# Two of four chunk pairs of each FFN's first product as seven block products instead of eight

## The chip, the cores and the metric

The kernel runs on one core of a Trainium2 chip. The metric is the device time of one execution in microseconds (us). Before the change it was 1284.43 us, the median of three runs (1284.11 to 1285.47).

## The reference

A decoder trunk of two layers on 256 tokens of width 1024, all in float32. Each layer is an FFN, a mixer of three branches, and a second FFN, each between two RMS norms:

```
def swiglu(h, wi, wo):
    gate, up = jnp.split(h @ wi, 2, axis=-1)
    return (jax.nn.silu(gate) * up) @ wo

for l in range(DEPTH):          # DEPTH = 2
    h = rms_norm(x, ffn1_pre_g[l])
    x = x + 0.5 * rms_norm(swiglu(h, ffn1_wi[l], ffn1_wo[l]), ffn1_post_g[l])
    h = rms_norm(x, mix_pre_g[l])
    y = hybrid_mixer(h, w_in[l], ...)
    x = x + rms_norm(y, mix_post_g[l])
    h = rms_norm(x, ffn2_pre_g[l])
    x = x + 0.5 * rms_norm(swiglu(h, ffn2_wi[l], ffn2_wo[l]), ffn2_post_g[l])
```

The change is in the product `h @ wi`, which stands in four FFN stages: (256 x 1024) by (1024 x 5632).

## The kernel before, in words

**Precision.** Every float32 operand of a large product is split into a high part (a cast to fp32r) and a low part (the operand minus the high part). A product is then three matmuls: high by high, low by high, high by low (`mm3`, L289 to L293). The activations' parts are `hh` and `hl`, made once a stage. The weights' parts are `hi` and `lo`, made as the weights come in: ScalarE casts (L146), VectorE subtracts (L147).

**Units.** The weights lie packed in 212 units of 128 x 2048 floats (1 MB) in the order of their use. A unit has two halves of 128 x 1024. `dma_to` loads a unit into one of two `raw` tiles, on the SyncE queue in order. `splitter` splits a half when one of eight ring places for hi and lo is free (`RING = 8`, `st_["free"]`), and `release` frees a place once PE's matmuls on that half have been issued. Two units at a stage boundary have tiles of their own (`place`, tag `q4`).

**An FFN stage.** The 5632 columns of wi are eleven chunks of 256 gate and 256 up columns. `wi(us, j, tt, rel)` makes chunk j for one half of the tokens (tt = 0 or 1, 128 tokens): `chunk512` multiplies the eight blocks of 128 rows, 24 matmuls of 128x512, into one PSUM bank of the pool `pmm`, which has two banks in turn. A coroutine then does silu on ScalarE (L349), the product with the up half on VectorE (L350), two transposes on PE (L237), and the split of the transposed result (L230 on ScalarE, L231 on VectorE) into `gT`. `wo(unit, j, tt, rel)` multiplies gT of chunk j with the rows of wo into two accumulators `acc`, 12 matmuls. In the middle of the stage the order is: wo of chunk j-2 for both token halves (one unit, freed in its second half), then wi of chunk j for both (two units, freed in the second). So a chunk is 72 matmuls of 128x512 and four transposes.

**Order.** The program is written by coroutines that run on a virtual clock (`Clock`): PE's instructions advance it, and the splitter and the gates yield a number of virtual microseconds. A scheduler then fixes each engine's order at build time from the program order, priorities (`tc.high_priority`) and its own estimates. On the chip each engine works through its list in order, and waits at an instruction whose inputs or whose tile are not there yet.

Of the kernel before, what the change touches and what calls it, by code (L numbers as in the profile page):

```python
# [15 lines left out]
P = 128  # L16
# [18 lines left out]
def f32(ap):  # L35
    return ap.bitcast(F32)
# [40 lines left out]
def trunk(ctx, tc, x, wpk, gains, lnp, wst, bst, consts, out, depth=DEPTH):  # L77
# [38 lines left out]
            tc.add_manual_dep(i.ins, lastdma[0].ins.name, NOSYNC, reason="load order")  # L116
        lastdma[0] = i

    def dma_to(n):
        while st_["dma"] < min(n, NU):  # L120
            u = st_["dma"]
            t = rp.tile([P, 2048], F32, tag="raw", name=f"raw{u}", bufs=2)
            for q in range(2 if u == 0 else 1):
                c = slice(1024 * q, 1024 * q + 1024) if u == 0 else slice(0, 2048)
                load(t[:, c], wpk[u][:, c])
            raws[u] = t
            st_["dma"] += 1

    def splitter():
        for u in range(NU):  # L130
            dma_to(u + 2)
            halves[u] = []
            for q in range(2):
                gate = place.get(u)
                while st_["free"] <= 0 if gate is None else not gate.on:
                    yield 0.2
                    gate = place.get(u)
                if gate is not None:
                    h = sp.tile([P, 1024], F32R, tag="q4", name=f"hi{u}_{q}", bufs=9)
                    lo = sp.tile([P, 1024], F32R, tag="q4", name=f"lo{u}_{q}", bufs=9)  # L140
                else:
                    st_["free"] -= 1
                    h = rp.tile([P, 1024], F32R, tag="hi", name=f"hi{u}_{q}", bufs=RING)
                    lo = rp.tile([P, 1024], F32R, tag="lo", name=f"lo{u}_{q}", bufs=RING)
                r = raws[u][:, 1024 * q:1024 * q + 1024]
                S.copy(h, r)  # L146
                V.tensor_sub(lo, r, f32(h))  # L147
                halves[u].append((h, lo))
                yield 1.2

    def wcols(u, c, n):
        h, lo = halves[u][c // 1024]
# [3 lines left out]
    def take(n):  # L156
        u0 = st_["pos"]
        st_["pos"] += n
        return list(range(u0, u0 + n))
# [23 lines left out]

    load(xs[0], x[0:P, :])
    gain(0)
    dma_to(1)
    load(xs[1], x[P:SEQ, :])
    dma_to(2)

    mB_ = cp.tile([P, 1152], BF16, tag="mB", name="mB")  # L190
    mB = [mB_[:, 768:1152], mB_[:, 0:768]]
# [94 lines left out]
            hready[tt] = f  # L286
            yield from prenorm(tt, nxt, f)

    def mm3(o, ah, al, bh, bl, first, stop, n=512):  # L289
        T.matmul(o, ah, bh, start=first, stop=False)  # L290
        T.matmul(o, ah, bl, start=False, stop=False)  # L291
        T.matmul(o, al, bh, start=False, stop=stop)  # L292
        ck.pe(3 * (n / 2400 + 0.003))  # L293

    def chunk512(us, tt, rel):
# [36 lines left out]
    def ffn(gi, nxt, first):  # L332
        acc = [None, None]
        gT, gf = {}, {}
        always = Flag()
        always.on = True
        for i in (32, 33):
            place[st_["pos"] + i] = always

        def wi(us, j, tt, rel):  # L340
            ps = chunk512(us, tt, rel)
            if tt == 0:
                t = sp.tile([P, 2, NT, 2, P], F32R, tag="t4", name=nm("gT"), bufs=5)
                gT[j] = (t[:, 0], t[:, 1])
            f = gf[j, tt] = Flag()

            def co():
                sg = w3_tile("sg")
                S.activation(sg[:, 0:256], ps[:, 0:256], AF.Silu)  # L349
                V.tensor_mul(sg[:, 0:256], ps[:, 256:512], sg[:, 0:256])  # L350
                yield 4.5 if (j, tt) == (0, 0) else 2.0
                to_T(sg, tt, 0, 2, *gT[j])
                yield 1.0
                f.on = True

            c = co()
            ck.start(c, 0.2)

        def wo(unit, j, tt, rel):
            ck.until(lambda: gf[j, tt].on)  # L360
            if acc[tt] is None:
                acc[tt] = [sc_tile("acc"), sc_tile("acc")]
            if j == NCH - 1:
                finish(tt, gi + 1, acc[tt], unit, *gT[j], 0, 2 * j, 2 * NCH, rel, 0.5, nxt)
            else:
                kunit(acc[tt], unit, *gT[j], tt, 0, 2 * j, 2 * NCH, rel)

        ua, ub = take(2), take(2)
        order = ((ua, 0, 0), (ua, 0, 1), (ub, 1, 0), (ub, 1, 1)) if first else \
                ((ua, 0, 0), (ub, 1, 0), (ua, 0, 1), (ub, 1, 1))  # L370
        for w, j, tt in order:
            wi(w, j, tt, tt == 1)
        for j in range(2, NCH - 1):
            if j == 3:
                if first:
                    load_consts()
                gain(gi + 1)
                gain(gi + 2)
            uo = take(1)[0]
# [444 lines left out]
```

## Time and profile before

| what | value |
|---|---|
| median of three runs | 1284.43 us |
| the profiled execution | 1285.66 us, its span 1284.0 us |
| PE busy | 1270.5 us (99%), 6428 matmuls |
| VectorE (DVE) busy | 763.0 us (59%) |
| ScalarE (ACT) busy | 645.5 us (50%) |
| DMA | 234.21 MB, mean 182 GB/s |
| mean granted TensorE clock | 0.999 |

The span is the time from the first to the last instruction of the profiled execution; the execution itself is 1.7 us longer. PE's matmuls overlap, so the busy time of one (about 0.39 us for 128x512) is not its cost: the distance of two start times is. The four FFN stages lie at about 12 to 190, 468 to 635, 635 to 823 and 1112 to 1278 us of the span, the mixers between them.

### The profile page before, as it was taken

How to read it: one execution, taken by the hardware profiler on the slowest of the kernel's cores; microseconds unless marked ns; L12 is line 12 of the kernel's file. 1: busy time of each engine (PE TensorE's matmuls, PEld its weight loads, DVE VectorE, ACT ScalarE, POOL GpSimd, SP SyncE). 2: the span in 40 equal slices, each digit the busy share in tenths (PEclk: the TensorE clock that was granted, in tenths of full speed). 3: DMA queues.
4: the chain of work that ended last, by engine and by line, in shares of the span. 5: the costliest groups of instructions: out<-in, count | busy, mean ns of one | idle time of the engine just before them, and what ended most of it. 6: DMA issues, size and time to landing. Idle time of an engine off the chain costs nothing.

```text
span 1284.0 us, 16016 instructions
## 1 busy us (share of the span) xinstructions
PE 1270.5 (99%) x6428; PEld 1059.2 (82%) x6428; DVE 763.0 (59%) x957; ACT 645.5 (50%) x896; POOL 34.5 (3%) x81
## 2 busy tenths in 40 slices
PE   8999999999999999999999999999999999999998
PEld 6888887998778888888888888789977788888886
DVE  5655557546765965555665555775466568655553
ACT  5544455445666454444554444654366655544442
POOL 0000001000000010000000000010000000000000
PEclk9999999999999999999999999999999999999999
DMA  7765554555335546555545555544543355455551
GB/s 246 262 225 192 176 189 163 197 190 190 116 125 193 200 161 230 197 182 182 179 177 212 185 194 197 197 170 166 213 167 131 131 197 201 160 212 178 185 179 50
DMA packets 34922, 234.21 MB, mean 182 GB/s; under 512 B 4128, under 2 KB 4256, under 8 KB 7840
## 3 DMA queue, kind: packets, MB, share of 16 engines
q1 hardware_dynamic: 34848, 233.20, 51.5%
q8 instruction: 50, 0.82, 0.3%
q14 instruction: 24, 0.20, 0.0%
HBM read 232.13 MB, written 1.05 MB: 182 GB/s over the span
## 4 chain that ended last, share of the span: by engine, by line
PE 95%; DVE 2%; ACT 2%; DMA 1%; issue 0%; SPq 0%; POOL 0%; DVEq 0%; POOLq 0%; ACTq 0%
PE mm L290 18%; PE mm L292 18%; PE mm L291 18%; PE acc L292 6%; PE acc L291 6%; PE acc L290 6%; PE qk L292 3%; PE qk L291 3%; PE qk L290 3%; PE tr L237 3%; PE pj L292 1%; PE pj L290 1%; PE pj L291 1%; PE wo L292 1%; PE wo L290 1%; PE wo L291 1%
## 5 line engine op out<-in xcount | busy, mean ns | idle before, releaser
L147 DVE TENSOR_TENSOR lo<-raw,hi 128x1024 fp32r<-128x1024 f32 x424 | 512.2, 1223 | 210.9 <-ACT hi L146 197.2
L146 ACT CAST hi<-raw 128x1024 fp32r<-128x1024 f32 x424 | 439.5, 1050 | 240.3 <-PE mm L292 86.2
L290 PE MATMUL mm<-hi,hh 128*128 128x512 f32 x1024 | 408.6, 399 | 1.4 <-ACT hh L230 1.4
L292 PE MATMUL mm<-hi,hl 128*128 128x512 f32 x1024 | 400.9, 391 | 0.2 <-DVE hl L231 0.2
L291 PE MATMUL mm<-lo,hh 128*128 128x512 f32 x1024 | 400.4, 391 | 0.0
L290 PEld LDWEIGHTS mm<-hi,hh 128*128 128x128 f32 x1024 | 193.1, 189 | 42.2 <-issue 2.7
L292 PEld LDWEIGHTS mm<-hi,hl 128*128 128x128 f32 x1024 | 192.8, 188 | 41.8 <-DVE hl L231 0.9
L291 PEld LDWEIGHTS mm<-lo,hh 128*128 128x128 f32 x1024 | 193.2, 189 | 36.7
L290 PE MATMUL acc<-hi,gT 128*128 128x512 f32 x352 | 140.9, 400 | 0.0
L292 PE MATMUL acc<-hi,gT 128*128 128x512 f32 x352 | 137.7, 391 | 0.0
L291 PE MATMUL acc<-lo,gT 128*128 128x512 f32 x352 | 137.3, 390 | 0.0
L349 ACT ACTIVATE sg<-mm 128x256 f32<-128x256 f32 x88 | 33.7, 383 | 160.8 <-PE mm L292 160.4
L350 DVE TENSOR_TENSOR sg<-mm,sg 128x256 f32<-128x256 f32 x88 | 37.0, 420 | 117.8 <-ACT sg L349 117.8
L290 PE MATMUL qk<-hh,hi 128*128 128x256 f32 x320 | 91.2, 285 | 0.0
L292 PE MATMUL qk<-hh,lo 128*128 128x256 f32 x320 | 90.6, 283 | 0.0
L291 PE MATMUL qk<-hl,hi 128*128 128x256 f32 x320 | 90.6, 283 | 0.0
L230 ACT CAST gT<-tr 128x256 fp32r<-128x256 f32 x88 | 32.4, 368 | 98.0 <-PE tr L237 98.0
L292 PEld LDWEIGHTS acc<-hi,gT 128*128 128x128 f32 x352 | 66.1, 188 | 14.1 <-DVE gT L231 0.2
L291 PEld LDWEIGHTS acc<-lo,gT 128*128 128x128 f32 x352 | 66.3, 188 | 12.5
L290 PEld LDWEIGHTS acc<-hi,gT 128*128 128x128 f32 x352 | 66.2, 188 | 12.3
L231 DVE TENSOR_TENSOR gT<-tr,gT 128x256 fp32r<-128x256 f32 x88 | 37.0, 421 | 63.1 <-ACT gT L230 63.0
L291 PEld LDWEIGHTS qk<-hl,hi 128*128 128x128 f32 x320 | 61.4, 192 | 0.1
(138 smaller groups left out, 1051.2 us busy)
## 6 DMA issues: line engine op xcount, KB each, us to landing
raw<-wpk SPq DMA_DIRECT2D x211, 1024.0 KB, 4.9
gain<-gains SPq DMA_DIRECT2D x12, 512.0 KB, 6.8
x<-x SPq DMA_DIRECT2D x2, 512.0 KB, 5.9
raw<-wpk SPq DMA_DIRECT2D x2, 512.0 KB, 6.9
ln<-lnp SPq DMA_DIRECT2D x4, 256.0 KB, 5.6
out<-x SPq DMA_DIRECT2D x4, 256.0 KB, 2.0
ws<-wst SPq DMA_DIRECT2D x2, 256.0 KB, 5.9
cst<-consts SPq DMA_DIRECT2D x1, 384.0 KB, 5.4
```

The costliest lines, as they stand in the source:

```text
L146: S.copy(h, r)
L147: V.tensor_sub(lo, r, f32(h))
L230: lasthi[0] = S.copy(h_out, src)
L231: V.tensor_sub(l_out, src, f32(h_out))
L237: T.transpose(tr[:, k * P:(k + 1) * P], src[:, k * P:(k + 1) * P], ident)
L290: T.matmul(o, ah, bh, start=first, stop=False)
L291: T.matmul(o, ah, bl, start=False, stop=False)
L292: T.matmul(o, al, bh, start=False, stop=stop)
L349: S.activation(sg[:, 0:256], ps[:, 0:256], AF.Silu)
L350: V.tensor_mul(sg[:, 0:256], ps[:, 256:512], sg[:, 0:256])
```

## The change

For the chunk pairs (4, 5) and (8, 9) of each stage the activations A (two token halves by two halves of the 1024 rows) and the weights B (two halves of the rows by two chunks) are taken as 2 x 2 blocks. The block product is made with Winograd's form of Strassen's scheme: seven products of 12 matmuls (`prod`) instead of eight. It needs four sums of activation blocks (`sums`, once a stage, on VectorE, then split), four sums of weight blocks a pair (made by the splitter on VectorE, eight sums of 128x1024, then split like weights), and five combinations of PSUM results (`post`, VectorE, 128x512). Product 1 is copied from PSUM by ScalarE, and the results of the bank of products 2 and 4 are added to that copy.

The loader follows a list `plan`. In a pair it has nine units to split where there were six: B11, T2, wo, B21, T3, T1, wo, T4, B22. B11 and B12 are loaded into four `q4` tiles, where T1 and T3 are made in place. T2 and T4 are made in two tiles of the tag `xn`. Block B22 is loaded twice. The activation sums have four `q4` tiles for the stage. In `pair7` two PSUM banks of `pmm` are used as b0 and b1; products 1 and 3, 2 and 4, 5 and 7 share a bank, product 6 has one.

```diff
+QUADS = (4, 8)
...
+            plan += [("w", c(j, q)) for j in range(2) for q in range(2)]
+            for j in range(2, NCH - 1, 2):
+                if j in qj:
+                    k = Quad({}, c(j, 0), c(j, 1), c(j + 1, 0), c(j + 1, 1))
...
+                    plan += [("B11", k), ("T2", k), ("w", w(j - 2)), ("B21", k), ("T3", k), ("T1", k),
+                             ("w", w(j - 1)), ("T4", k), ("B22", k)]
...
+        def stream(key, u, first=False):
+            while len(ring) >= 2 and ring[-2] not in done:
+                yield
+            ring.append(key)
             t = rp.tile([P, 2048], F32, tag="raw", name=f"raw{u}", bufs=2)
...
+            if kind == "B11":
+                f = k.ffn
+                if "f" not in f:
+                    f["f"] = [sp.tile([P, 1024], F32, tag="xn", name=nm("wf"), bufs=2) for _ in WQ]
+                for q in range(2):
+                    V.tensor_add(f["a"][q], f["a"][q], f["b"][q])
+                    V.tensor_add(f["f"][q], f["a"][q], raw[k][q])
+                    yield 1.2
+            elif kind == "T2":
+                for q in range(2):
+                    V.tensor_add(k.ffn["b"][q], k.ffn["b"][q], raw[k][q])
+                    yield 0.6
+                done.add(k)
+            elif kind == "B21":
+                for q in range(2):
+                    V.tensor_add(k.ffn["f"][q], k.ffn["f"][q], raw[n][q])
+                    yield 0.6
...
+        def sums(ss):
+
+            def full(tt, k):
+                t = w3_tile("sA")[:, 0:512].rearrange("p (k t) -> p k t", t=P)
+                V.tensor_add(t, f32(hh[:, tt, k:k + 4, :]), f32(hl[:, tt, k:k + 4, :]))
+                return t
+
+            def split(a):
+                o = sp.tile([P, 2, 4, P], F32R, tag="q4", name=nm("sA"), bufs=9)
+                S.copy(o[:, 0], a)
+                V.tensor_sub(o[:, 1], a, f32(o[:, 0]))
+                ss.append(o)
...
+        def prod(ps, ah, al, it, first):
+
+            for k in range(4):
+                have(it, k // 2)
+                h, l = wcols(it, k * 512, 512)
+                mm3(ps, ah[:, k, :], al[:, k, :], h, l, first and k == 0, k == 3, go_on=not first)
+                if k % 2:
+                    release(it)
...
+            def post(o, a, b, op):
+                with tc.high_priority(offset=HOT):
+                    V.tensor_tensor(o, a, b, op=op)
...
+            def chunk(jj, tt, a, b, op):
+                c = w3_tile("cc")
+                post(c[:, 0:512], a, b, op)
+                out(c[:, 0:256], c[:, 256:512], jj, tt, c[:, 0:256])
+
+            b0, b1 = mm(), mm()
+            prod(b0, *A(0, 0), take(1)[0], True)
+            S.copy(p1, b0)
+            prod(b1, *s2, take(1)[0], True)
+            post(u2, b1, p1, ALU.add)
+            wo2(j - 2)
+            prod(b0, *A(0, 4), take(1)[0], False)
+            out(b0[:, 0:256], b0[:, 256:512], j, 0, w3_tile("sg")[:, 0:256])
+            prod(b1, *s3, take(1)[0], False)
+            post(u3, b1, p1, ALU.add)
+            b0 = mm()
+            prod(b0, *s1, take(1)[0], True)
+            chunk(j + 1, 1, b0, u3, ALU.subtract)
+            wo2(j - 1)
+            b1 = mm()
+            prod(b1, *A(1, 4), take(1)[0], True)
+            chunk(j, 1, b1, u3, ALU.add)
+            prod(b0, *s4, take(1)[0], False)
+            chunk(j + 1, 0, b0, u2, ALU.subtract)
```

`out` is the gate of `wi` (silu, product, transposes, split) as a function of its own. The consts and two gains are loaded at chunk 4 instead of 3.

How the order moves, first on PE at the end of the last pair before chunk 10 in the second FFN. `mm` are banks of `pmm` (every second number is the same bank), `sA` the sums of activations, `tr` a transposed tile, `cc` a combined chunk. Before:

```order
L290 MATMUL mm_373_4952<-hi100_1_4859,hh_94 128x512
L291 MATMUL mm_373_4952<-lo100_1_4860,hh_94 128x512
L292 MATMUL mm_373_4952<-hi100_1_4859,hl_95 128x512
L290 MATMUL mm_376_4999<-hi101_0_4871,hh_94 128x512
L291 MATMUL mm_376_4999<-lo101_0_4872,hh_94 128x512
L292 MATMUL mm_376_4999<-hi101_0_4871,hl_95 128x512
```

and now:

```order
L383 MATMUL mm_400_5048<-hi112_1_5057,sA_350_4217 128x512
L384 MATMUL mm_400_5048<-lo112_1_5058,sA_350_4217 128x512
L385 MATMUL mm_400_5048<-hi112_1_5057,sA_350_4217 128x512
L383 MATMUL mm_408_5171<-hi113_0_5069,hh_94 128x512
L384 MATMUL mm_408_5171<-lo113_0_5070,hh_94 128x512
L385 MATMUL mm_408_5171<-hi113_0_5069,hl_95 128x512
L330 MATMUL tr_409_5175<-ident_73,cc_406_5143 128x128 x2
```

Before, chunk 10 took the bank of mm_371, which was filled one whole product before mm_373. Now mm_408 takes the bank of mm_400 (mm_405, product 6, has the other), which is filled by the three rows just above it.

Second, VectorE at the same place, before (chunk 9 and the splits of chunk 10; `sg` is a gate):

```order
L231 TENSOR_TENSOR gT_365_4830<-tr_368_4854,gT_365_4830 128x256
L147 TENSOR_TENSOR lo101_0_4872<-raw101_4813,hi101_0_4871 128x1024
L350 TENSOR_TENSOR sg_369_4881<-mm_366_4831,sg_369_4881 128x256
L147 TENSOR_TENSOR lo101_1_4885<-raw101_4813,hi101_1_4884 128x1024
L231 TENSOR_TENSOR gT_365_4830<-tr_370_4902,gT_365_4830 128x256
```

and now, from the combination of product 6 on:

```order
L536 TENSOR_TENSOR cc_406_5143<-mm_405_5120,u_393_4912 128x512
L218 TENSOR_TENSOR lo115_0_5137<-raw103_5094,hi115_0_5136 128x1024
L470 TENSOR_TENSOR cc_406_5143<-cc_406_5143 128x256
L218 TENSOR_TENSOR lo115_1_5151<-raw103_5094,hi115_1_5150 128x1024
L536 TENSOR_TENSOR cc_407_5169<-mm_400_5048,u_393_4912 128x512
L324 TENSOR_TENSOR gT_399_5024<-tr_409_5175,gT_399_5024 128x256
L470 TENSOR_TENSOR cc_407_5169<-cc_407_5169 128x256
```

Two combinations (L536) stand among the splits (L218); the second, cc_407, is what reads product 7 out of its bank.

Third, VectorE in the first FFN, at chunk 2 (unit 9 is the last of chunk 3, `wa` holds B11 of the first pair). Before:

```order
L147 TENSOR_TENSOR lo8_1_404<-raw8_344,hi8_1_403 128x1024
L350 TENSOR_TENSOR sg_33_435<-mm_30_399,sg_33_435 128x256
L147 TENSOR_TENSOR lo9_0_445<-raw9_371,hi9_0_444 128x1024
L147 TENSOR_TENSOR lo9_1_460<-raw9_371,hi9_1_459 128x1024
L231 TENSOR_TENSOR gT_31_430<-tr_34_454,gT_31_430 128x256
```

and now:

```order
L218 TENSOR_TENSOR lo8_1_427<-raw8_344,hi8_1_426 128x1024
L504 TENSOR_TENSOR sA_41_444<-sA_41_444,sA_34_392 128x512
L218 TENSOR_TENSOR lo9_0_477<-raw9_375,hi9_0_476 128x1024
L218 TENSOR_TENSOR lo9_1_492<-raw9_375,hi9_1_491 128x1024
L218 TENSOR_TENSOR lo10_0_504<-wa_29_377,hi10_0_503 128x1024
L488 TENSOR_TENSOR sA_33_389<-sA_28_363,sA_33_389 128x512
L488 TENSOR_TENSOR sA_38_419<-sA_34_392,sA_38_419 128x512
L488 TENSOR_TENSOR sA_40_441<-sA_27_361,sA_40_441 128x512
L488 TENSOR_TENSOR sA_42_459<-sA_41_444,sA_42_459 128x512
L443 TENSOR_TENSOR sg_45_467<-mm_39_422,sg_45_467 128x256
L443 TENSOR_TENSOR sg_47_513<-mm_44_463,sg_47_513 128x256
```

The gate of chunk 2's first token half stood ahead of the splits of unit 9; now it stands behind them, behind a half of B11 and behind the four splits of activation sums.

## Rows read from the trace of the kernel before

**Rows 1.** Page, part 1: busy us of each engine, share of the span, instructions.
```profile
PE 1270.5 (99%) x6428; PEld 1059.2 (82%) x6428; DVE 763.0 (59%) x957; ACT 645.5 (50%) x896; POOL 34.5 (3%) x81
```

**Rows 2.** Page, part 4: chain that ended last, share of the span by engine.
```profile
PE 95%; DVE 2%; ACT 2%; DMA 1%; issue 0%; SPq 0%; POOL 0%; DVEq 0%; POOLq 0%; ACTq 0%
```

**Rows 3.** Waits of PE: us in total, times, longest.
```profile
PE tr L237 <- DVE sg L350: 2.0, 3, 0.7
PE tr L237 <- DVE xn L258: 1.6, 1, 1.6
PE mm L290 <- ACT hh L230: 1.4, 1, 1.4
```

**Rows 4.** Timeline of PE in an output product: start, us, engine, line, operation.
```profile
516.14 0.39 PE L290 MATMUL acc<-hi,gT 128*128 128x512 f32 x1
...
518.86 0.39 PE L290 MATMUL acc<-hi,gT 128*128 128x512 f32 x1
```

**Rows 5.** Stretches: length, busy us of PE, PEld, DVE, ACT, POOL; PEclk, DMA, GB/s.
```profile
60.00:70.00 10.00, 10.00 (x47) 8.24 (x46) 5.09 (x8) 3.99 (x7) 0.00 (x0) 1.00 0.90 342
...
468.00:635.00 167.00, 167.00 (x759) 137.73 (x758) 89.75 (x106) 76.71 (x107) 0.86 (x2) 1.00 0.54 190
...
510.66:527.48 16.82, 16.82 (x77) 13.87 (x76) 8.87 (x10) 7.62 (x11) 0.00 (x0) 1.00 0.55 189
```

**Rows 6.** Timeline of ACT in the second FFN; in brackets idle time, and its end.
```profile
528.84 1.05 ACT L146 CAST hi<-raw 128x1024 fp32r<-128x1024 f32 x1 [0.98 <-PE mm L292]
530.20 1.05 ACT L146 CAST hi<-raw 128x1024 fp32r<-128x1024 f32 x1 [0.30 <-PE mm L292]
```

**Rows 7.** Groups by line and shape: busy us, mean ns | idle before, releaser.
```profile
L147 DVE TENSOR_TENSOR lo<-raw,hi 128x1024 fp32r<-128x1024 f32 x424 | 512.2, 1223 | 210.9 <-ACT hi L146 197.2
L146 ACT CAST hi<-raw 128x1024 fp32r<-128x1024 f32 x424 | 439.5, 1050 | 240.3 <-PE mm L292 86.2 <-PE qk L291 61.7 <-DMA raw<-wpk 41.2
...
L231 DVE TENSOR_TENSOR gT<-tr,gT 128x256 fp32r<-128x256 f32 x88 | 37.0, 421 | 63.1 <-ACT gT L230 63.0
L350 DVE TENSOR_TENSOR sg<-mm,sg 128x256 f32<-128x256 f32 x88 | 37.0, 420 | 117.8 <-ACT sg L349 117.8
L349 ACT ACTIVATE sg<-mm 128x256 f32<-128x256 f32 x88 | 33.7, 383 | 160.8 <-PE mm L292 160.4 <-DVE gT L231 0.3
...
L230 ACT CAST gT<-tr 128x256 fp32r<-128x256 f32 x88 | 32.4, 368 | 98.0 <-PE tr L237 98.0
...
L230 ACT CAST hh<-tr 128x512 fp32r<-128x512 f32 x32 | 18.5, 586 | 30.3 <-PE tr L237 30.3
...
L271 DVE TENSOR_TENSOR yn<-acc,gain 128x512 f32<-128x512 f32 x16 | 11.0, 689 | 16.4 <-ACT sq L270 16.4
...
L690 DVE TENSOR_TENSOR mg<-mg,gate 128x512 f32<-128x512 f32 x16 | 10.6, 682 | 0.0
...
L655 ACT COPY gate<-mm 128x512 f32<-128x512 f32 x12 | 7.0, 583 | 6.9 <-PE mm L292 6.9
```

**Rows 8.** Page, part 6: DMA issues, KB each, median us from issue to landing.
```profile
raw<-wpk SPq DMA_DIRECT2D x211, 1024.0 KB, 4.9
```

**Rows 9.** Timeline of DVE in the first FFN: two splits back to back.
```profile
45.91 2.36 DVE L147 TENSOR_TENSOR lo<-raw,hi 128x1024 fp32r<-128x1024 f32 x2 [0.58 <-ACT hi L146]
```

**Rows 10.** Timeline of ACT in the first FFN.
```profile
41.56 1.05 ACT L146 CAST hi<-raw 128x1024 fp32r<-128x1024 f32 x1 [3.04 <-DMA raw<-wpk]
...
49.16 0.38 ACT L349 ACTIVATE sg<-mm 128x256 f32<-128x256 f32 x1 [2.33 <-PE mm L292]
50.52 1.05 ACT L146 CAST hi<-raw 128x1024 fp32r<-128x1024 f32 x1 [0.98 <-PE mm L292]
```

**Rows 11.** Stretches at a norm boundary and at the end, columns as in rows 5.
```profile
190.00:198.00 8.00, 7.33 (x38) 5.72 (x37) 7.01 (x9) 4.62 (x8) 1.01 (x2) 1.00 0.33 109
...
1276.00:1284.00 8.00, 1.60 (x8) 0.98 (x6) 2.79 (x4) 1.38 (x4) 0.86 (x2) 0.77 0.18 66
```

More of the change, by code (lines that the diff above doesn't have):

```diff
@@ L122, in dma_to, with loader @@
+    NI = len(plan)
+    WQ = (slice(0, 1024), slice(1024, 2048))
+    done, raw = set(), {}
+    def loader():
+        ring = []
+        def stream(key, u, first=False):
+            while len(ring) >= 2 and ring[-2] not in done:
+                yield
+            ring.append(key)
             t = rp.tile([P, 2048], F32, tag="raw", name=f"raw{u}", bufs=2)
-            for q in range(2 if u == 0 else 1):
-                c = slice(1024 * q, 1024 * q + 1024) if u == 0 else slice(0, 2048)
+            raw[key] = [t[:, c] for c in WQ]
+            for c in WQ if first else (slice(0, 2048),):
@@ L125, in dma_to @@
                 load(t[:, c], wpk[u][:, c])
-            raws[u] = t
-            st_["dma"] += 1
+        for n, (kind, k) in enumerate(plan):
+            if kind == "w":
+                yield from stream(n, k, n == 0)
+            elif kind == "B11":
+                while k.prev and not k.prev.t1:
+                    yield
+                f = k.ffn
+                if not f:
+                    for t in "ab":
+                        f[t] = [sp.tile([P, 1024], F32, tag="q4", name=nm("w" + t), bufs=9) for _ in WQ]
+                raw[n] = f["a"]
+                for t, u in ((f["a"], k.u11), (f["b"], k.u12)):
+                    for q, c in enumerate(WQ):
+                        load(t[q], wpk[u][:, c])
+                yield from stream(k, k.u22)
+            elif kind in ("B21", "B22"):
+                yield from stream(n, k.u21 if kind == "B21" else k.u22)
+            yield
@@ L129, in splitter, with ready @@
+    ld = loader()
+    def ready(n, kind, k):
+        if kind[0] == "T":
+            raw[n] = k.ffn[{"T1": "a", "T2": "f", "T3": "b", "T4": "f"}[kind]]
+        return n in raw and (kind != "B11" or k in raw)
     def splitter():
-        for u in range(NU):
-            dma_to(u + 2)
-            halves[u] = []
+        for n, (kind, k) in enumerate(plan):
+            while not ready(n, kind, k):
+                next(ld)
+            halves[n] = []
             for q in range(2):
-                gate = place.get(u)
+                gate = place.get(n)
@@ L151, in wcols @@
+            done.add(n)
+            for _ in range(3):
+                next(ld, None)
     def wcols(u, c, n):
@@ L366, in wo, with out, co @@
                 kunit(acc[tt], unit, *gT[j], tt, 0, 2 * j, 2 * NCH, rel)
+        def out(ps_a, ps_b, j, tt, sg):
+            if j not in gT:
+                t = sp.tile([P, 2, NT, 2, P], F32R, tag="t4", name=nm("gT"), bufs=5)
+                gT[j] = (t[:, 0], t[:, 1])
+            f = gf[j, tt] = Flag()
+            def co():
+                S.activation(sg, ps_a, AF.Silu)
+                V.tensor_mul(sg, ps_b, sg)
+                yield 2.0
+                to_T(sg, tt, 0, 2, *gT[j])
+                yield 1.0
+                f.on = True
+            ck.start(co(), 0.2)
@@ new lines, in sums @@
+        def sums(ss):
[8 more added lines that the diff above has]
+                ss.append(o)
+            t, s1 = full(1, 0), full(1, 4)
+            yield 1.5
+            V.tensor_sub(s1, t, s1)
+            split(s1)
+            s2 = full(0, 0)
+            yield 2.2
+            V.tensor_sub(t, s2, t)
+            V.tensor_sub(s2, s1, s2)
+            split(s2)
+            yield 2.2
+            split(t)
+            s4 = full(0, 4)
+            yield 2.2
+            V.tensor_add(s4, s4, s2)
+            split(s4)
@@ L368, in ffn @@
+        ss = []
         ua, ub = take(2), take(2)
@@ L372, in ffn @@
             wi(w, j, tt, tt == 1)
+        ck.start(sums(ss), 0.2)
         for j in range(2, NCH - 1):
-            if j == 3:
+            if j == 4:
                 if first:
```

75 lines of the change are left out of this document (58 added, 17 removed).

## The prediction

> **What bounds the kernel now.** First the page's table of engines [rows 1]: PE is busy 99% of the span, VectorE 59%, ScalarE 50%. Then the chain that ended last [rows 2]: 95% of it is PE. Then the waits of PE [rows 3]: the three largest entries are 2.0, 1.6 and 1.4 us. So the time is the number of matmuls times their spacing, plus a short start and tail. The spacing is read from the start times in the PE timeline [rows 4]: twelve 128x512 matmuls from 516.14 to 518.86, so 2.72 us for twelve, 0.2267 each (the 0.39 us of one matmul overlaps the next).
>
> Next the room on the other engines in an FFN, from the table by stretches [rows 5]: one output chunk takes 16.82 us, in which PE is always busy, VectorE works 8.87 us and ScalarE 7.62. Last, who holds whom: the casts that start a weight split wait for PE [rows 6], because all eight ring places are full and PE has to free one. So weights are ready four units before their use. That lead is what the change spends.
>
> **What it removes.** A pair of chunks has eight block products of 12 matmuls; the new pair has seven. Two pairs in each of four FFN stages: 8 x 12 = 96 matmuls, 96 x 0.2267 = 21.8 us (2.72 a pair). Transposes and output products stay. A pair goes from 33.6 us (two chunks of rows 5) to 30.9.
>
> The Trainium skill has smaller spacings: "TensorE: Matmul & The Clock Gate", section "Back-to-back issue gap", gives about 131 ns sustained for 512 columns, by which the gain would be 12.6 us. The trace disagrees, with 0.2267 us where PE never waits [rows 4], and the row decides.
>
> **What it adds, per pair.** Seven weight blocks are split where four were: six more casts (1.05 us) and six more subtractions (1.22) [rows 7]. Eight sums of 128x1024 fp32 weights on VectorE are not in the trace. Bounds: 0.68 (the 128x512 sum L690, as if size cost nothing) and 1.36 (that row twice); the subtraction L147 has the same shape and number of operands, so 1.22. Five combinations of a 128x512 PSUM result: 0.69 (L271). One copy of the first product on ScalarE: 0.58 (L655). VectorE in a pair: 9 units x 2 x 1.22 + 8 x 1.22 + 5 x 0.69 + 4 x (0.42 + 0.42) = 22.0 + 9.8 + 3.4 + 3.4 = 38.6 us against 30.9 of PE; before it was 17.7 against 33.6. ScalarE: 18 x 1.05 + 0.58 + 4 x (0.38 + 0.37) = 22.5, which fits. Once a stage the token sums cost VectorE 12 x 0.68 = 8.2 us and ScalarE 4 x 0.59. A whole stage gives VectorE 12 x 1.22 + 16 x 1.22 + 10 x 0.69 + 8.2 = 49 us more; in the stretch 468 to 635 of rows 5 it has 89.8 of 167, so 139 of about 162: 86%.
>
> **Does PE wait for weights?** I keep a ledger from the start of the chunk before a pair to the pair's last product: PE 16.8 + 30.9 = 47.7 us. PE frees 3 + 9 units in it, so VectorE makes 24 splits (29.3), 8 sums (9.8), 5 combinations (3.4) and about six gates with their transposed halves (5.0): 47.5. It breaks even over the stretch. Inside, it falls behind where the four sums after the first block meet the two splits beside them: six operations, 7.3 us, in a 5.4 us output product. Going through the new order by hand with these durations I find it at most about 5 us late. The lead is four units, 10.9 us where all four are product blocks (2.72 each) and more with an output unit. So weights don't stall PE, and the following chunks (8.87 of 16.8) refill the ring. The second block's weights must also follow the sums through a load: block 21 takes the place of block 22 once VectorE has used that, and needs 4.9 us to land [rows 8]; by the ledger VectorE waits 1 to 2 us for it, inside the lead. Block 22 is loaded twice, 1 MB a pair; the queue has brought 342 GB/s where 189 is usual here [rows 5, 8].
>
> **Where PE does wait.** VectorE works in the order it was given, so a combination that PE needs stands behind the splits placed ahead of it. Three places:
> 1. After the second pair's product 7, PE goes straight on with the last chunk's first product, which takes the PSUM bank that product 7 just filled; before, that bank had been read out one 5.4 us product earlier. From the end of product 6 VectorE has a combination, a split, a gate, a split and the last combination: 0.69 + 1.18 + 0.42 + 1.18 + 0.69 = 4.2 us (1.18 is half of two splits back to back, 2.36 us [rows 9]). PE arrives after 2.72: it waits 1.5 us in three stages. In the first stage the order has one split less and no gate: 0.7 us after product 7 and its signal, 0.8. Together 5.3.
> 2. Inside a pair product 5 reuses the bank of product 3 after one product, where before there were two, and the transposes of combined chunks stand at fixed places. By the ledger the waits are 0.3 us (second FFN, first pair) and 0.9 (first FFN, second pair): 0.6 a pair, 4.8 in all. Bounds: nothing, and 2.7 a pair (two splits and a late gate).
> 3. In the first FFN the ring is not yet full: casts wait up to 3.04 us for loads [rows 10]. There the order puts two splits of unit 9 and the four token splits ahead of a gate whose product ended at 49.16 [rows 10]; it comes near 58.5, the transpose that needs it near 58.4. Then the B sums are late: product 5 waits about 2.3 us for the gate of product 3. With 0.7 for the first: 3 us on top; bounds 0 and 6.
>
> Sum against the profiled execution, 1285.66 us (span 1284.0 and 1.7 around it): -21.8 + 5.3 + 4.8 + 3.0 = -8.7, or 1277.0. The median of the timed runs lies 1.2 us below the profiled one, so 1275.7; ledger waits are rounded up in most places (1.22 for splits that follow each other at 1.18), and I say 1275.
>
> **Rivals.**
> A. All hidden. VectorE idles 7.9 us of each plain chunk [rows 5], and if the waits of places 2 and 3 vanish, 5.3 remain: 1284.4 - 16.5 = 1268. Against it: VectorE breaks even at best in the stretch around a pair.
> B. VectorE's order costs more than the products. Place: the gates and combinations in the pair. Price: one split more ahead of each of the three combinations that release PE is 3.7 us a pair instead of 0.6, 8 x 3.1 = 25 us more: 1300. It decides from 2.72 us of waits a pair (21.8 in all). For it: 38.6 us of VectorE work in a 30.9 us pair; against it: the ring's lead and the slack on both sides. Slower by a little, about 1290, is its likelier form.
> C. Waits eat just the gain (about 20 us): 1282 to 1287.
> D. The clock. Granted clock is 1.00 through waits of up to 1.6 us [rows 3, 11], but 0.77 in the last 8 us, where PE works only 1.60 [rows 11]: part of it is spent at 1.2 GHz. If each pair had a wait that long, and one product behind it ran at half speed, 8 x 2.7 = 22 us come back: 1297. My waits are 0.3 to 2.3 us. The Trainium skill has the rule ("TensorE: Matmul & The Clock Gate", section "HAM oscillation — how this bites in real kernels"): an idle PE is throttled, and the cold start is paid each time. By that rule this rival needs idle stretches as at the end of the trace; the trace agrees that short ones cost nothing.
>
> That the change doesn't remove the matmuls is excluded: 12 fewer stand in each of eight pairs.
>
> **How the numbers follow.** Forecast (1269 to 1282) 0.62; A 0.12; C 0.09; B 0.14; D 0.03. A difference of 0.2%, 2.6 us, is about what a measurement of this kernel can tell from none. Faster: forecast and A, 0.74. Same: C, 0.09. Slower: B and D, 0.17. The range leaves out the best tip of A and the worst of B and D: 1265 to 1288.
>
> **What would show it.** PE with 96 matmuls fewer at the same spacing. VectorE near 960 us (763 + 4 x 49) and near 100% in the pairs. PE waits for DVE of some 13 us in total, largest after product 7 of the second pair of each stage (1 to 2 us, bank of the last chunk) and in the first FFN near 60 and 90 us. No PE wait for lo or hi of weights. A wait for weights, waits over 2.7 us a pair, or a lower granted clock in the FFN stages would make the prediction wrong.

## The result and the profile after

The changed kernel takes 1264.47 us (median of four runs, 1263.61 to 1265.89), the kernel before 1284.38 beside it: a ratio of 0.9841 (95% interval 0.9827 to 0.9855), 19.9 us less. The prediction was 1275 with a range from 1265 to 1288: the direction is right, the gain is a little over twice the 9.4 us that were forecast, and the time lies just below the range. The profiled execution took 1265.89 us with a span of 1263.5, at a mean granted clock of 0.999.

Part 1 of the page of the kernel after, which answers to [rows 1]:

```profile
PE 1248.7 (99%) x6332; PEld 1040.4 (82%) x6332; DVE 930.6 (74%) x1157; ACT 701.8 (56%) x968; POOL 34.6 (3%) x81
```

The 96 matmuls are gone. VectorE (DVE) has 168 us more, where the prediction had 196.

The waits of PE in the kernel after (us in total, times, longest), to be held against [rows 3]:

```profile
PE tr L330 <- DVE sg L443: 3.6, 5, 0.9
PE tr L330 <- DVE xn L351: 1.5, 1, 1.5
PE warm L925 <- POOL ident masks.py:199: 1.4, 1, 1.4
PE mm L383 <- ACT hh L323: 1.1, 1, 1.1
```

The gates (sg) have 1.6 us and two waits more than before. What the prediction had expected above all is missing: no PE wait for a combination (cc or u, L536), none for a PSUM bank, none for weights. The list shows only time in which nothing runs on PE, and the 0.39 us record of a matmul covers the first part of a gap. So I also went through the distances of all start times against the 0.2267 us of [rows 4]. In the stages only three places have more than 0.12 us over it, 2.1 us in all (timeline of PE in the kernel after; start, us; in brackets idle time and what ended it):

```profile
40.42 0.44 PE L330 MATMUL tr<-ident,sg 128*128 128x128 f32 x2 [0.68 <-DVE sg L443]
...
58.52 0.44 PE L330 MATMUL tr<-ident,sg 128*128 128x128 f32 x2 [0.86 <-DVE sg L443]
...
168.87 0.41 PE L330 MATMUL tr<-ident,cc 128*128 128x128 f32 x2
```

By start times they are 0.84, 1.01 and 0.25 us. At the boundaries between stages PE waits as before, 0.8 to 0.9 us each. So -21.8 + 2.1 = -19.7 us, against a measured difference of -19.9. (The spans differ by 20.5: in the profiled execution of before ten of the first FFN's matmuls still came 0.43 us apart, in that of after four, which is 1.2 us by itself. The granted clock reads 1.00 in both stretches, so what spaces them there stays open.)

Stretches of the kernel after, as [rows 5] (length, busy us of PE, PEld, DVE, ACT, POOL; PEclk, DMA, GB/s): the second pair of the second FFN, and that whole stage.

```profile
575.75:606.46 30.71, 30.71 (x140) 25.26 (x139) 26.51 (x30) 20.31 (x26) 0.00 (x0) 1.00 0.55 182
462.00:629.00 167.00, 167.00 (x760) 137.54 (x760) 136.38 (x161) 95.02 (x132) 1.87 (x4) 1.00 0.59 205
```

A pair takes 30.7 us, as forecast (30.9), and PE is never idle in it. But VectorE works 26.5 us in it, 86%, and not near 100%: only 30 of a pair's 39 operations on VectorE fall into it, so the others are done before it begins, and each costs VectorE less time than I had reckoned (below).

Costs of the new operations, by line and shape, as [rows 7] (busy us, mean ns):

```profile
L226 DVE TENSOR_TENSOR wa<-wa,wb 128x1024 f32<-128x1024 f32 x16 | 19.2, 1217 | 0.0
...
L536 DVE TENSOR_TENSOR cc<-mm,u 128x512 f32<-128x512 f32 x24 | 16.4, 684 | 1.8 <-PE mm L385 1.7
...
L550 ACT COPY u<-mm 128x512 f32<-128x512 f32 x8 | 4.7, 585 | 4.0 <-PE mm L385 4.0
```

They agree with the 1.22, 0.69 and 0.58 of the prediction. Those are lengths of records, though, not what an operation costs its engine. The timeline of VectorE in a pair of the kernel after:

```profile
593.45 0.69 DVE L536 TENSOR_TENSOR u<-mm,u 128x512 f32<-128x512 f32 x1
594.05 0.41 DVE L324 TENSOR_TENSOR gT<-tr,gT 128x256 fp32r<-128x256 f32 x1
594.38 1.22 DVE L218 TENSOR_TENSOR lo<-raw,hi 128x1024 fp32r<-128x1024 f32 x1
595.51 0.68 DVE L536 TENSOR_TENSOR cc<-mm,u 128x512 f32<-128x512 f32 x1
596.12 1.22 DVE L218 TENSOR_TENSOR lo<-raw,hi 128x1024 fp32r<-128x1024 f32 x1
597.25 0.42 DVE L470 TENSOR_TENSOR cc<-cc 128x256 f32<-128x256 f32 x1
```

The next one starts 0.60 us after a 128x512 operation, 0.33 after a 128x256 and 1.13 after a 128x1024, some 0.08 before the record ends. Before the change it was the same, and [rows 9] had it in plain sight: two splits take 2.36, so the second adds 2.36 - 1.22 = 1.14. I had taken half of 2.36.

### The profile page after: what moved, and what is told of

Same layout as the page of the kernel before. It is cut to its first block, busy times and chain, and to the rows that moved or that the text cites. A ratio compares the mean times of both kernels' runs of the same rounds, so it can differ in the third digit from the quotient of the medians.

```text
span 1263.5 us, 16239 instructions
## 1 busy us (share of the span) xinstructions
PE 1248.7 (99%) x6332; PEld 1040.4 (82%) x6332; DVE 930.6 (74%) x1157; ACT 701.8 (56%) x968; POOL 34.6 (3%) x81
## 4 chain that ended last, share of the span: by engine, by line
PE 91%; DVE 4%; DMA 2%; ACT 2%; issue 1%; POOL 0%; SPq 0%; DVEq 0%; POOLq 0%; ACTq 0%
PE mm L383 16%; PE mm L385 16%; PE mm L384 16%; PE acc L385 6%; PE acc L384 6%; PE acc L383 6%; PE qk L384 3%; PE qk L383 3%; PE qk L385 3%; PE tr L330 3%; DMA raw<-wpk 2%; DVE lo L218 2%; PE pj L385 1%; PE pj L383 1%; PE pj L384 1%; ACT hi L217 1%
## 5 line engine op out<-in xcount | busy, mean ns | idle before, releaser
L218 DVE TENSOR_TENSOR lo<-raw,hi 128x1024 fp32r<-128x1024 f32 x392 | 470.2, 1221 | 166.2 <-ACT hi L217 160.8
L217 ACT CAST hi<-raw 128x1024 fp32r<-128x1024 f32 x392 | 402.9, 1049 | 266.2 <-DMA raw<-wpk 72.4
L383 PE MATMUL mm<-hi,hh 128*128 128x512 f32 x864 | 344.8, 399 | 1.1 <-ACT hh L323 1.1
L385 PE MATMUL mm<-hi,hl 128*128 128x512 f32 x864 | 338.4, 392 | 0.2 <-DVE hl L324 0.2
L384 PE MATMUL mm<-lo,hh 128*128 128x512 f32 x864 | 338.3, 392 | 0.0
L383 PEld LDWEIGHTS mm<-hi,hh 128*128 128x128 f32 x864 | 162.8, 188 | 36.0 <-issue 2.7
L385 PEld LDWEIGHTS mm<-hi,hl 128*128 128x128 f32 x864 | 162.6, 188 | 35.5 <-DVE hl L324 0.9
L384 PEld LDWEIGHTS mm<-lo,hh 128*128 128x128 f32 x864 | 163.1, 189 | 30.9
L383 PEld LDWEIGHTS qk<-hh,hi 128*128 128x128 f32 x320 | 61.5, 192 | 0.1
L385 PEld LDWEIGHTS qk<-hh,lo 128*128 128x128 f32 x320 | 61.5, 192 | 0.0
```

Of the source, the lines that this page charges most:

```text
L383: T.matmul(o, ah, bh, start=first, stop=False, skip_group_check=go_on)
L384: T.matmul(o, ah, bl, start=False, stop=False, skip_group_check=go_on)
L385: T.matmul(o, al, bh, start=False, stop=stop, skip_group_check=go_on)
```

## The experiments

What they had to tell apart: is the wait of place 1 (the last chunk behind product 7) missing because of the bank, because of the order, or because VectorE is early; and how much room does VectorE have in a pair? In the runs on VectorE's room (5, 6 and 10) theory A is the ledger with 1.14, 0.60 and 0.34 us, theory B that of the prediction. All ratios are to the kernel before, where the changed kernel has 0.9841.

**1. Chunk 10 in product 7's bank.** In the built program chunk 10's first product doesn't lie in product 7's bank, against what is said with the order of PE's rows ahead of the prediction (mm_408 and mm_400). The times show it in all four stages: PE starts chunk 10 at 167.03, 606.45, 789.24 and 1228.76, and the combination that reads product 7 ends only at 168.39, 608.58, 791.12 and 1230.68. With two banks that leaves the bank of product 6. That the pool gives out the bank which is read out first fits this; it is inferred. Here `pair7` returns `b0` and chunk 10 uses it:

```diff
-            wi(us, NCH - 1, tt, tt == 1)
+            wi(us, NCH - 1, tt, tt == 1, None if tt else b0)
```

> Chunk 10's first product is written into the bank of product 7, as the prediction had assumed; in the changed kernel it lies in the bank of product 6. All else is the same. Theory A (the wait of place 1 exists, and was only put on the wrong bank): PE waits for the last combination of the second pair, which in the changed kernel ends at 168.39, 608.58, 791.12 and 1230.68, while PE's next matmul stands at 167.03, 606.46, 789.24 and 1228.76. So waits of 1.4, 2.1, 1.9 and 1.9 us, 7.3 in all, shown as PE mm waiting for DVE cc: 1264.5 + 7.3 = 1271.8 us. By the prediction's own figure 5.3: 1269.8. Rival B (the wait isn't there, since VectorE comes sooner than the ledger has it): no such PE wait, 1264.5 us.

Measured 1267.85 us, 0.9864 (0.9849 to 0.9878), some 3.4 us over the changed kernel, and neither theory. PE's order had changed: the scheduler knows at build time that this product must wait, and put matmuls of an output product ahead of it (five in the first stage, seven in the others). The list of waits has none for the combination. By start times the four places together cost 0.9 us more than in the changed kernel, 1.5 us fell at a boundary at 450 to 464 us, and 1.2 at the start.

**2. The same, with the first output product held behind it** by an order dependency on chunk 10's last matmul (`held[0]`):

```diff
+        if held[1]:
+            for m in ms:
+                tc.add_manual_dep(m.ins, held[0].ins.name, NOSYNC, reason="after chunk 10")
...
+                if tt == 0 and i == 0:
+                    held[1] = True
                 wo(uo[i], NCH - 3 + i, tt, tt == 1)
+                held[1] = False
```

> As the run with chunk 10 in product 7's bank, and the first output product after chunk 10's first product is held behind it in PE's order, as it stands in the changed kernel: in the run before, the scheduler had put seven matmuls of it ahead. Theory A (what hid the wait there was the scheduler's filling): PE now waits for the last combination of the second pair: 1.4, 2.1, 1.9 and 1.9 us by the changed kernel's times, 7.3 in all, 1268 to 1273 us, and the waits show as idle time ahead of a matmul into mm. Rival B (VectorE is simply early enough): no such wait, 1264 to 1266 us.

Measured 1268.01 us, 0.9870 (0.9854 to 0.9887). That is the lower edge of theory A's range, but not its reason: the list of waits has 0.3 us for the combination where A had 7.3. Now the scheduler put matmuls of chunk 10's second token half ahead, which has the other bank (again five and seven), and the four places cost 1.3 us more than in the changed kernel. It filled the wait again.

**3. All held.** Every later product of the stage is held behind chunk 10's first:

```diff
+            held[1] = True
             for i in range(3):
                 wo(uo[i], NCH - 3 + i, tt, tt == 1)
+        held[1] = False
```

> Chunk 10's first product in product 7's bank, and now every later output product and chunk 10's second product are held behind it, so that PE's order at this place is that of the changed kernel (only the transposes of the combined chunk 9 stand ahead). Theory A (the wait of place 1 is real on this bank, and in the runs before the scheduler filled it with other matmuls): PE's first matmul of chunk 10 waits for the last combination: by the changed kernel's times 1.4, 2.1, 1.9 and 1.9 us less the 0.1 to 0.2 of two transposes, 6 to 7 us in all, 1269 to 1273 us. By the prediction's figures 1.5 three times and 0.8: 5.3 us, 1269.8. Rival B (no wait): 1264 to 1266 us.

Measured 1272.98 us, 0.9901 (0.9885 to 0.9918): theory A. The wait is there, four times. First its row in the waits of PE, then the place in the second FFN in the timelines of PE and of DVE:

```profile
PE mm L385 <- DVE cc L544: 5.3, 4, 1.4
```

```profile
607.38 0.39 PE L387 MATMUL mm<-hi,sA 128*128 128x512 f32 x1
608.19 0.41 PE L330 MATMUL tr<-ident,cc 128*128 128x128 f32 x2 [0.42 <-DVE cc L478]
609.92 0.47 PE L385 MATMUL mm<-hi,hh 128*128 128x512 f32 x1 [1.32 <-DVE cc L544]
```

```profile
607.96 1.22 DVE L218 TENSOR_TENSOR lo<-raw,hi 128x1024 fp32r<-128x1024 f32 x1
609.09 0.68 DVE L544 TENSOR_TENSOR cc<-mm,u 128x512 f32<-128x512 f32 x1
```

The combination that reads product 7 stands behind a split, ends at 609.77, and PE goes on at 609.92. 5.3 us of idle time is the very figure of the prediction, for a bank that the kernel doesn't use there. That the sums agree so well is partly luck: the four waits are 1.28 to 1.37 us each, where the prediction had 0.8 once and 1.5 three times. (By start times the four places cost 8.5 us, as much as the median rose: the transposes wait too, and in the second FFN the granted clock was 0.57 for a while, some 1.5 us.) In the changed kernel the two do not meet (PE, then DVE, same place):

```profile
606.23 0.39 PE L385 MATMUL mm<-hi,sA 128*128 128x512 f32 x1
606.45 0.39 PE L383 MATMUL mm<-hi,hh 128*128 128x512 f32 x1
```

```profile
606.77 1.22 DVE L218 TENSOR_TENSOR lo<-raw,hi 128x1024 fp32r<-128x1024 f32 x1
607.90 0.68 DVE L536 TENSOR_TENSOR cc<-mm,u 128x512 f32<-128x512 f32 x1
```

Chunk 10 begins at 606.45, and product 7 is read only at 607.90.

**4. No weight sums.** All four lines of sums are left out, as this one, and T2 and T4 are split from B12's tile; the splits stay.

```diff
-                    V.tensor_add(f["a"][q], f["a"][q], f["b"][q])
```

> The eight sums of weight blocks a pair are left out: the products run on single blocks of weights, so the output isn't the reference's. VectorE has 9.1 us less in each pair. Theory A (the sums are hidden: PE waits for nothing that they delay): only the first FFN's waits could go, 1262 to 1265 us. Theory B (the ledger: VectorE at break-even, so the sums cost PE a part of their time that is spread too finely for the list of waits): 1255 to 1261 us.

Measured 1264.89 us, 0.9841 (0.9827 to 0.9856): no difference to the changed kernel, theory A. The first row of its page, against 930.6 us of VectorE in the changed kernel:

```profile
PE 1248.3 (99%) x6332; PEld 1039.5 (82%) x6332; DVE 863.9 (68%) x1093; ACT 704.0 (56%) x968; POOL 34.1 (3%) x81
```

PE's waits stayed at 40 and 58 us. The sums, the largest new item, cost PE nothing.

**5 and 6. More sums.** The second sum of B11's turn is made three times, or five times, in place of once:

```diff
-                    V.tensor_add(f["f"][q], f["a"][q], raw[k][q])
+                    for _ in range(3):
+                        V.tensor_add(f["f"][q], f["a"][q], raw[k][q])
```

> The sum of block 22's half onto T1 is made three times instead of once: four more 128x1024 sums on VectorE a pair, right after the splits of B11. The result is the same. Theory A (1.14 us each): 4.6 us more in the stretch of a chunk and a pair, 43.6 + 4.6 = 48.2 against 47.7 of PE, inside the lead: PE waits 0 to 1 us a pair, 1264 to 1272 us. Theory B (the ledger, 1.22 each, already at break-even): 47.5 + 4.9 = 52.4, 4.7 us behind in every pair, of which gates and transposes pass on 2 to 4.7: 1280 to 1302 us.

Measured 1281.61 us, 0.9973 (0.9961 to 0.9985): in B's range, not in A's.

> As the run with four more sums, with five times in place of three: eight more 128x1024 sums a pair. Theory A: 9.1 us more, 52.7 against 47.7, 5 us behind at the end of each pair, which the lead of the weights still covers but the gates and combinations do not: PE waits 1 to 4 us a pair, 1272 to 1297 us. Theory B: 57.3, 9.6 us behind in each pair: 1300 to 1340 us. If the time stays at 1264.5 neither ledger says what VectorE's room is.

Measured 1328.68 us, 1.0341 (1.0319 to 1.0363): B's range again. So the ledger with the smaller terms forecast too little in both. The totals alone don't say why (run 4 tells that the sums as they stand cost nothing, which would also be so just at break-even). The trace of the run with four more sums shows what both ledgers leave out (DVE, then PE, at the first pair of the third FFN):

```profile
693.96 6.90 DVE L228 TENSOR_TENSOR wf<-wa,raw 128x1024 f32<-128x1024 f32 x6
...
705.32 0.42 DVE L444 TENSOR_TENSOR sg<-mm,sg 128x256 f32<-128x256 f32 x1
```

```profile
703.04 1.10 PE L384 MATMUL acc<-hi,gT 128*128 128x512 f32 x4
705.79 0.44 PE L331 MATMUL tr<-ident,sg 128*128 128x128 f32 x2 [1.65 <-DVE sg L444]
```

The burst of sums and the splits that follow it stand ahead of the gate of the chunk before the pair, and PE needs that gate in the output product. In the changed kernel this gate ended at 691.82 and its transpose came at 692.09: 0.27 us of room, where the ledger over the whole stretch has 4.

```profile
691.40 0.42 DVE L443 TENSOR_TENSOR sg<-mm,sg 128x256 f32<-128x256 f32 x1
```

```profile
692.09 0.38 PE L330 MATMUL tr<-ident,sg 128*128 128x128 f32 x2
```

With 4.6 us more of sums ahead of it PE waits 1.6 us there, in four of the eight pairs. They are those with the least room: in the changed kernel the same gate has 0.27 to 1.17 us at these four, and 1.61 to 2.19 us at the four that don't wait. By start times the four waits are 7.1 of the 17.1 us that this run lost against the changed kernel; waits for casts inside the stages (2.5), more at the stage boundaries (2.7) and matmuls 0.43 us apart (2.7) have a part too, and the rest is not placed. With eight more sums PE waits 2.4 to 5.1 us for weights in all eight pairs. Each further us on VectorE then costs PE 47.1 / 36.5 = 1.3 us: some 12 of the 47.1 us are matmuls 0.43 us apart behind such waits, in stretches whose granted clock is 0.50 to 0.61.

**7. The same amount elsewhere.** Four subtractions a pair are made twice, after the second halves of B21, T1, T4 and B22.

```diff
                 V.tensor_sub(lo, r, f32(h))
+                if kind in ("T1", "T4", "B22", "B21") and q == 1:
+                    V.tensor_sub(lo, r, f32(h))
```

> Four subtractions 128x1024 more on VectorE a pair, as many us as in the run with four more sums (4.6 a pair), but one each after the second half of B21, T1, T4 and B22 (the subtraction is made twice, the result is the same). Theory P (what counts is what stands behind the extra work: there a gate of the chunk before, which PE transposes; here nothing that PE soon needs): PE waits 0 to 0.5 us a pair, 1264 to 1269 us. Theory T (VectorE's total in the pair decides): as the run with the four sums together, 1278 to 1285 us.

Measured 1291.39 us, 1.0052 (1.0037 to 1.0067): worse than the burst, and both theories missed. The trace divides it. Inside the stages the start times give 7.1 us over 0.2267 (2.1 in the changed kernel), so 0.6 a pair, near theory P. At three stage boundaries it is 19.1 us (2.6 in the changed kernel). There the scheduler made another order: one more split stands between the residual sums of the first token half, and PE began its last matmul before the wait 5.2 us after that half's first square, where the changed kernel has 8.4 us of work there. Waits of PE in this run:

```profile
PE tr L332 <- DVE xn L353: 12.1, 6, 3.3
PE mm L385 <- ACT hh L325: 2.9, 4, 0.9
PE tr L332 <- DVE sg L445: 2.0, 4, 0.9
```

So an added instruction also moves places that it has nothing to do with. Some 4 us of this run I could not place, and how much of its boundary cost is order and how much a later VectorE stays open.

**8. Token sums later in the first FFN.**

```diff
-        ck.start(sums(ss), 0.2)
+        ck.start(sums(ss), 6.0 if first else 0.2)
```

> In the first FFN the token sums start 6 virtual us later, so that a gate of chunk 2 no longer stands behind their four splits. Theory (place 3 of the prediction): the wait at 58.5 us for the gate (0.86, or 1.0 by the distance of matmul starts) goes, and nothing else: 1263 to 1264.5 us, which the time can hardly tell, the trace can. Rival: the gate is late because of the loads of B11 and B12, and the wait stays within 0.3 us of 0.86.

Measured 1265.51 us, 0.9848 (0.9834 to 0.9863), not to be told from the changed kernel. The idle time at 58 us fell from 0.86 to 0.32 us, that at 40 us by start times from 0.84 to 0.24, and a new wait of 0.50 for a gate came at 117: neither theory, and no gain.

**9. One pair a stage.**

```diff
-QUADS = (4, 8)
+QUADS = (8,)
```

> Only pair (8, 9) of each stage is taken as seven products: 48 matmuls fewer than before, 10.9 us. Theory A (each pair gives its 2.72 us and costs PE nothing but the first FFN's gate): 1284.4 - 10.9 + 0 to 2 = 1273.5 to 1275.5 us. Theory B (the waits belong to the first pair or to both together): if a pair costs waits that the changed kernel hides elsewhere, more than 1277.

Measured 1275.56 us, 0.9927 (0.9912 to 0.9942): theory A, 0.06 us above its range. Four pairs at 2.72 us are 10.9; the first FFN's waits are there with one pair too (0.35 and 0.94 us by start times), which leaves 9.6, and 9.1 was measured.

**10. Three pairs a stage.**

```diff
-QUADS = (4, 8)
+QUADS = (4, 6, 8)
```

> Chunk pair (6, 7) of each stage is taken as seven products as well: three pairs in a row, 48 matmuls fewer than in the changed kernel, or 10.9 us of PE at 0.2267 us. Theory A (an operation of VectorE costs its distance to the next, 1.14 us for 128x1024, 0.60 for 128x512, 0.34 for 128x256, and not the 1.22, 0.69 and 0.42 of its own record): a pair is 26 x 1.14 + 5 x 0.60 + 8 x 0.34 = 35.4 us of VectorE against 30.9 of PE; three in a row put it 13.4 us behind, against a lead of 10.9 and some 8 us of idle time in the chunk ahead: waits of 0 to 2 us a stage, 1254 to 1262 us. Theory B (the prediction's ledger): 38.6 a pair, 23 us behind after three, so some 4 us for weights and as much for gates in each stage: 1270 to 1290 us.

Measured 1309.44 us, 1.0195 (1.0173 to 1.0217): slower than before, beyond even theory B. The first pair of a stage runs free, the waits begin within the second. Waits of PE:

```profile
PE mm L384 <- DVE lo L218: 14.2, 17, 1.8
PE tr L330 <- DVE cc L470: 9.2, 5, 2.7
PE tr L330 <- DVE xn L351: 6.9, 7, 2.1
```

The ground is one that rival B of the prediction names: work on VectorE over PE's in pair after pair, 35.4 against 30.9 us, once the lead is spent. But its largest wait, for split weights, is not among rival B's places, and VectorE is not the only cause. The cast of block 11 (`wa`) now waits for its load, which hardly happens with two pairs. Waits of ACT, in this run and in the changed kernel:

```profile
ACT hi L217 <- DMA wa<-wpk: 11.2, 5, 3.5
```

```profile
ACT hi L217 <- DMA wa<-wpk: 0.5, 1, 0.5
```

In the second FFN VectorE stands idle behind such a cast, and PE's longest wait of the stage follows (ACT, DVE, PE):

```profile
579.42 1.05 ACT L217 CAST hi<-wa 128x1024 fp32r<-128x1024 f32 x1 [3.53 <-DMA wa<-wpk]
```

```profile
581.08 0.42 DVE L324 TENSOR_TENSOR gT<-tr,gT 128x256 fp32r<-128x256 f32 x1 [2.85 <-ACT gT L323]
```

```profile
585.30 0.69 PE L330 MATMUL tr<-ident,cc 128*128 128x128 f32 x2 [2.41 <-DVE cc L470]
```

In the three stages where the cast waits 2.4 to 3.5 us, PE waits 2.3 to 2.8 us (by start times) at this place; in the fourth, where the cast doesn't wait, 1.0. Beyond that the two engines wait for each other in turn (VectorE for a transposed gate, PE for a split behind it), which no ledger of sums contains, and the clock falls. How much of the loss is VectorE's work and how much the loads stays open.

**11 and 12. The weight sums on GpSimd**, with two pairs and with three; all four lines of sums as this one:

```diff
-                    V.tensor_add(f["a"][q], f["a"][q], f["b"][q])
+                    G.tensor_add(f["a"][q], f["a"][q], f["b"][q])
```

> All eight sums of weight blocks a pair are made by GpSimd in place of VectorE. No trace here shows such a sum on GpSimd; the nearest row is its 128x512 AFFINE_SELECT at 0.64 us, twice that is 1.3. Theory A (sums hidden on either engine): VectorE 930 - 78 = 852 us, 1262 to 1266 us if a sum takes at most some 2.5 us on GpSimd (20 us of 30.9 a pair). Rival: a sum takes 3 us or more, or slows VectorE's operations beside it: T2 is late, PE waits for its weights, 1275 to 1310 us.

Measured 1343.91 us, 1.0456 (1.0441 to 1.0472): the rival, and worse than its range. What PE waits for, though, are gates of VectorE (59 us in all), not the weights as the rival had it.

> Three pairs a stage as in the run with three pairs, but with the weight sums on GpSimd. Theory A (there VectorE was the bound, at 35.4 us a pair against 30.9): now 26.3 us a pair, and PE gets its weights: 1264.5 - 10.9 = 1253.6, up to 1260 us with some waits. Rival (the loads of B11 and B12, which can start only when T1 of the pair before has been split, are the bound): waits stay, 1280 to 1310 us.

Measured 1409.32 us, 1.0966 (1.0950 to 1.0983): waits as its rival has it, but far over its range and not for its reason. ScalarE's casts wait 0.9 us for loads of `wa`, and 125 us for sums on GpSimd. So this run doesn't tell VectorE's work from the loads in run 10. Waits of ACT:

```profile
ACT hi L217 <- POOL wf L227: 124.9, 24, 7.0
```

In the run with two pairs a sum takes 2.4 to 3.2 us on GpSimd by the means of its lines, and the splits of one line on VectorE grow from 1.22 to 1.92 on average (groups by line; busy us, mean ns, idle before):

```profile
L231 POOL TENSOR_TENSOR wb<-wb,raw 128x1024 f32<-128x1024 f32 x16 | 50.7, 3180 | 0.0
...
L226 POOL TENSOR_TENSOR wa<-wa,wb 128x1024 f32<-128x1024 f32 x16 | 38.8, 2424 | 339.7 <-DVE lo L218 297.4 <-DMA wb<-wpk 42.4
```

```profile
L218 DVE TENSOR_TENSOR lo<-wf,hi 128x1024 fp32r<-128x1024 f32 x32 | 61.5, 1922 | 55.6 <-ACT hi L217 55.2
```

No version beat the changed kernel.

## Why the prediction was wrong

The sum was -21.8 + 5.3 + 4.8 + 3.0. The first term holds; the waits were 2.1 us in place of 13.1.

**Place 1 (5.3 us, found: 0). This is the step that failed**: "the last chunk's first product, which takes the PSUM bank that product 7 just filled". I read banks off the numbers of tile names, as if two banks went strictly in turn. By the times the chunk has the other bank in all four stages (run 1); product 6's combination stands ahead of product 7's, so a pool that gives out what is released first would do this. The working behind it was sound in the main: with the bank as assumed and PE's order held, run 3 shows 5.3 us of idle time. And even with that bank the build would have filled the wait with other matmuls (runs 1 and 2: 0.9 and 1.3 us in all), a second thing that the step left out.

**Place 2 (4.8 us, found 0.25).** The step was sized by the ledger, and the ledger's terms were too large. With the distances in place of the lengths, the 47.5 us of VectorE become 24 x 1.14 + 8 x 1.14 + 5 x 0.60 + 12 x 0.34 = 43.6, against 47.7 of PE: 4 us early where I had break-even. The trace agrees: in five of the eight pairs the gate that frees product 5's bank ends 1.23 us before product 5 begins, in two others 0.50 and 0.21. At one of the five (DVE's gate, then PE's first matmul of product 5):

```profile
590.68 0.42 DVE L470 TENSOR_TENSOR sg<-mm,sg 128x256 f32<-128x256 f32 x1
```

```profile
592.33 0.39 PE L383 MATMUL mm<-hi,sA 128*128 128x512 f32 x1
```

The corrected ledger isn't a sure guide either: it forecast runs 5, 6 and 10 too low, since it holds neither where in the order the work stands nor the loads. I had noticed that splits follow each other at less than their length, and gave it 0.7 us in the sum. The Trainium skill has the rule ("Vector Engine (DVE) Microarchitecture Reference", section "5.2 Measured stream behaviour on trn2"): 1.0417 ns a column and some 75 ns an instruction, measured there on 32-bit integers, so an estimate of 1.14 us for 1024 columns and 0.61 for 512. The trace agrees, with 1.13 and 0.60.

**Place 3 (3.0 us, found 1.85).** The gate at 58.5 us came late as forecast (0.7; measured 1.0). The 2.3 us of product 5 near 90 us did not: in that one pair product 5 has product 4's bank, by the times, so it didn't need the gate at all: it began at 89.48, before the gate at 90.30. The 0.84 us at 40.42 was not forecast; there a gate stands behind two splits whose loads came late.

**What held.** 96 matmuls at 0.2267 us, a pair of 30.7 us, no wait for weights, the operations' lengths, the wait for block 21's load (4.1 us on VectorE, longest 1.9, hidden), a clock of 0.999. VectorE was forecast near 960 us and near 100% in a pair; it had 930.6 us and 86%.

Rival A came nearest, and its reason held: VectorE has enough idle time. But it kept the 5.3 us of place 1, the one term that was wrong through and through. Rivals B and D are not far off: four more sums a pair give most of the gain back (0.9973), and a third pair makes it a loss.

## What to carry to other kernels

Reckon an engine's room by the distance of start times in a busy stretch, not by the length of its records: here 0.08 us an operation, 49 operations in a chunk and a pair, made 4 us of slack. Before a wait on a buffer is charged, find out which buffer the allocator really gives, and whether the build orders other work into the wait. And room over a stretch is not room at each instruction: the same kernel had 4 us over a chunk and a pair and 0.27 us at one gate, and with four more sums a pair in front of that gate PE waited there in four of eight pairs, 7.1 of the 17.1 us that were lost.

## What the runs showed of the hardware

The clock. After a wait of PE the granted clock can fall to its lower level, 1.2 GHz, for some us. The run with four more sums has four waits of 1.6 to 1.7 us for a gate. The first of them in the timeline of PE, then the 4.50 us up to its end and the 3.90 us behind it (columns as above):

```profile
74.52 0.44 PE L331 MATMUL tr<-ident,sg 128*128 128x128 f32 x2 [1.65 <-DVE sg L444]
```

```profile
70.02:74.52 4.50, 2.79 (x12) 1.64 (x11) 4.50 (x6) 2.55 (x3) 0.00 (x0) 1.00 0.00 0
74.50:78.40 3.90, 3.88 (x11) 3.11 (x12) 2.56 (x3) 0.37 (x1) 0.00 (x0) 0.56 0.96 298
```

The other is the wait that ends at 705.79, shown with run 5:

```profile
701.29:705.79 4.50, 2.85 (x13) 1.93 (x12) 4.50 (x6) 2.83 (x4) 0.00 (x0) 1.00 0.00 0
705.79:709.69 3.90, 3.90 (x18) 3.24 (x19) 2.88 (x4) 0.96 (x2) 0.00 (x0) 1.00 0.93 288
```

PE did nearly the same up to the end of either wait: 2.79 and 2.85 us busy of 4.50. Behind the first the clock was 0.56 and matmuls came 0.43 us apart, 1.7 us in all; behind the second it stayed at 1.00, and so it did behind the other two. Why the price differs stays open. In the run with three pairs a wait of 2.41 us was followed by 3.9 us at 0.57, in the run with the spread subtractions one of 3.29 by 6.5 us at 0.51. So rival D's mechanism exists at waits of this size, if not each time; the changed kernel has none of more than 0.86 us of idle time inside its stages. The reading behind rival D, a granted clock of 1.00 through waits of up to 1.6 us, was too sure: of the waits of [rows 3] only one of 0.7 us lies in the first stretch of [rows 11], and the longer ones, 1.6 and 1.4 us, stand at the start of the span, where matmuls then came 0.43 us apart.

GpSimd and VectorE slow each other: in run 11 a split of VectorE that met no sum of GpSimd took 1.21 to 1.23 us (428 of them), one that lay almost wholly beside a sum 2.44 us in the median and up to 3.36 (24 of them); a sum took some 2.4 us where VectorE was idle, and up to 3.4 beside its work. The Trainium skill has it ("SBUF — State Buffer", section "Who interferes with whom"): a VectorE instruction with two inputs in SBUF contends with a GpSimd instruction that reads SBUF. The trace agrees.
